# Moving operands of a decoder layer's products read column by column in turn from two areas of their tile

## The chip, the cores and the metric

The kernel runs on one core of a Trainium2 chip. A core has a matrix engine (PE in the profile; its weight loads are listed apart as PEld), a vector engine (DVE), a scalar engine (ACT), GpSimd (POOL), and a sync engine (SP) that issues most of the transfers between the chip's memory and the core's own. The metric is the device time of one execution in microseconds (us). The kernel before takes 2058.32 us, the median of three runs (2055.09, 2058.32, 2060.36).

## The reference

One layer of a decoder for 512 tokens of width 2048, everything in float32:

```
mod = SiLU(c) @ W_ada + b_ada            # six vectors: shift1, scale1, gate1, shift2, scale2, gate2
h   = RMSNorm(x) * (1 + scale1) + shift1
u   = h @ W_in                           # B, C, H of the convolution; q; k and v of three branches; gates
y_conv = B * causal_depthwise_conv3(C * H)
y_attn = gated sum of compressed, selected and sliding-window attention (8 heads, 2 key/value heads)
x   = x + gate1 * ([RMSNorm(y_conv) | RMSNorm(y_attn)] @ W_out)
h   = RMSNorm(x) * (1 + scale2) + shift2
x   = x + gate2 * (relu(h @ W1)^2 @ W2)  # W1: 2048 x 8192, W2: 8192 x 2048
out = RMSNorm(x)
```

## The kernel before

Activations lie with features on the 128 partitions and tokens along the row of a partition. A float32 product is made of three products in the format float32r: each operand is split into a rounded part and the rest (`wh` and `wl` of the weights, index 0 and 1 of the tokens' tiles), and `mm3` issues high x high, high x low and low x high into the same accumulator. The second argument of `nc.tensor.matmul` is the stationary operand, loaded by an instruction of its own (LDWEIGHTS) before each product; the third is the moving operand, which is streamed past it.

There are three stages, and the profile names their accumulators:

- Front, accumulators `ps`: the projections of `h` by `W_in`, 512 tokens wide, each weight blob of 1024 columns giving 8 x 3 products. The loop over `steps` is the first part. Its tokens `h` (features 0 to 6) and `h_m` (7 to 15) are made while it runs: for each block of 128 features DVE forms two modulation columns by four dot products with `w_ada` blobs (`wa`), scales the tokens and subtracts (`low`). Then follow `project`, `compress` (moving operand 256 columns of a compression weight, stationary operand 66 columns), `values` (moving operand 268 weight columns) and `queries`.
- Attention, accumulators `s`, `pt`, `pv`, and `pw` for the convolution's half of `W_out` (`out_conv`, 512 tokens), which fills gaps between them.
- Output projection and feed-forward, accumulators `pf`. Both feed-forward products use a scheme of seven products instead of eight over halves of 256 tokens; `run` issues 8 x 3 products, 256 tokens wide, per operand. The weight operands are rounded by ACT and their rest is formed by DVE in the tiles `hl`, three in a ring, one operand ahead of PE. In the second feed-forward product the results are added into `xt` (`gather`); when the sixth of eight feature groups is done, `add_residual` multiplies `xt` by gate2 and adds the stored residual, and the last two groups are added with the gate (`update`).

Every instruction passes through `Order.record`, so the profile puts all of them on one line, L123; they are told apart by tile names. `Order.emit` plans each of the three stages with a list scheduler: a price for each instruction (`Order.price`), due times from the order of PE's products, and the readiness of operands; it writes the instructions out in planned order, and each engine then runs its own in that order. For a float32r product the price is `max(0.109, 0.0015 + n * self.column)` us for n columns, with 0.000441 as `column` in the front and the feed-forward, and 0.000453 in attention.

In the built program the tiles of tokens start at multiples of 128 bytes of a partition's row. The weight tiles `wh`, `wl` of the front and `kw` of the output projection do so too; the tiles `hl`, `gt` and `sg`, where they hold feed-forward weights, start 64 bytes off such a multiple.

Of the kernel before, what the change touches and what calls it, by code (L numbers as in the profile page):

```python
# [16 lines left out]
P = 128  # L17
# [25 lines left out]
M_SH1, M_SC1, M_G1, M_SH2, M_SC2, M_G2 = range(6)  # L43


class Order:
# [47 lines left out]
    def price(self, eng, op, out, ins, kw):  # L94
# [199 lines left out]
def hybrid_layer(ctx: ExitStack, tc: tile.TileContext, a, out):  # L294
# [146 lines left out]
    def row_bcast(bank, total, width, dst):  # L441
# [5 lines left out]
        if dst is not None:  # L447
            nc.scalar.activation(dst, ps[:, :n * P], AF.Copy)
# [97 lines left out]
    def rope(dst, ps):  # L546
# [7 lines left out]
        nc.vector.tensor_tensor(out=dst, in0=t[:, 0], in1=t[:, 1], op=OP.add)  # L554
        yield 0.65

    def rope_split(dst, ps, scale):
        t = temp(name="rs2")
        yield from rope(t, ps)
# [69 lines left out]
    for s, (name, k) in enumerate(steps[:-1]):  # L629
# [7 lines left out]
        if s < 3:  # L637

            for ww, j in ((wh, 0), (wl, 0), (wh, 1)):
                for n, c in enumerate(cols):  # L640
                    nc.tensor.matmul(ps[n], ww[:, c], hs[k][:, j], start=first and ww is wh and j == 0,
                                     stop=last and j == 1)
# [89 lines left out]
    def project(src, tiles):  # L732
        ps = bank()
        for half in range(2):
            wh, wl = ahead.pop() if ahead else weights(src(half))
            for j in range(8):
                k = half * 8 + j
                s = slice(j * P, (j + 1) * P)
                mm3(ps, wh[:, s], wl[:, s], tiles[k][:, 0], tiles[k][:, 1], k == 0, k == NK - 1)
# [16 lines left out]
    def compress(which, src):  # L756
# [26 lines left out]
        for blk in range(8):  # L783
            wh, wl = w
            hi, lo = parts[blk // 4]
            for j in range(4):
# [4 lines left out]
                mm3(pc[:66, :256], ch, cl, wh[:, s], wl[:, s], l == 0, l == 31)  # L791
# [91 lines left out]
    def values(g):  # L883
        pv = [both[i] for i in (4, 6, 7, 5)] if g else [bank() for _ in range(NQ)]
        for n, blk in enumerate(range(4) if g == 0 else (2, 3, 1, 0)):
# [3 lines left out]
            for j in range(4):  # L889
                k = blk * 4 + j  # L890
                s = slice(j * 268, (j + 1) * 268)
                for t in range(NQ):
                    c = slice(t * P, (t + 1) * P)
                    mm3(pv[t][:, :268], hs[k][:, 0, c], hs[k][:, 1, c], wh[:, s], wl[:, s],
                        n + j == 0, (n, j) == (3, 3))
# [44 lines left out]
    def queries(g):  # L940
        pq = [bank() for _ in range(NR)]
        for k in range(NK):
# [4 lines left out]
            for n in range(NR):  # L947
                s = slice((k % 2 * NR + n) * P, (k % 2 * NR + n + 1) * P)
                mm3(pq[n], wh[:, s], wl[:, s], hs[k][:, 0], hs[k][:, 1], k == 0, k == NK - 1)
# [51 lines left out]
    def out_conv(m):  # L1001
        if m % 4 < 2:
            x1.append(slot(name="x1")[:, :1024].rearrange("p (c j t) -> p c j t", c=2, j=2))
            order.keep(x1[-1])
            for j in range(2):
                nc.sync.dma_start(out=x1[-1][:, :, j],
                                  in_=a["xt"][m // 4 * 2 + j, :, m % 2].rearrange("p (c t) -> p c t", c=2))
        ps = next(pws)
        wh, wl = oc.pop() if oc else weights(a["w_oc"][m])
        with lane(2):  # L1010
            for k in range(8):
                s = slice(k * P, (k + 1) * P)
                mm3(ps, wh[:, s], wl[:, s], mix[k][:, 0], mix[k][:, 1], k == 0, k == 7)
# [4 lines left out]
    def attention(g, qb):  # L1018
# [86 lines left out]
        for r in range(NR):  # L1105
            nc.scalar.activation(ya[g * NR + r][:, qc], pv[:, r * P:(r + 1) * P], AF.Copy)
# [28 lines left out]
    row_bcast(lambda: next(turned), tot, 1024, ra)  # L1135
# [99 lines left out]
    for k in range(8):  # L1235
        wh, wl = oa[k] if k < 2 else hilo(hl_tile(16), raw_blob(a["w_oa"][k]))
        for i in range(8):
            s = slice(i * P, (i + 1) * P)
            mm3(pm[i], wh[:, s], wl[:, s], mixa[k][:, 0], mixa[k][:, 1], k == 0, k == 7)
# [18 lines left out]
    def late_out(hf):  # L1258
        ps = []
        for i in range(8):  # L1260
# [3 lines left out]
            for k in range(8):  # L1264
                mm3(ps[-1][:, halves[i % 2]], columns(wh, k), columns(wl, k), mixa[k][:, 0, halves[hf]],
                    mixa[k][:, 1, halves[hf]], k == 0, k == 7)
# [373 lines left out]

def _shape_constants(np):
# [8 lines left out]
    i = np.arange(P)  # L1650
# [9 lines left out]
def _layouts(np, x, c, w_ada, b_ada, norm1_g, w_in, conv_w, conv_b, cmp_pe_k, cmp_pe_v, cmp_w1_k,  # L1660
# [10 lines left out]
    def quads(w):  # L1671
# [5 lines left out]
    d["xt"] = x[0].T.reshape(NK // 2, 2, P, T).transpose(0, 2, 1, 3)  # L1677
# [12 lines left out]
          .reshape(4, 4, P, 268).transpose(0, 2, 1, 3).reshape(4, P, BLOB) for g in range(NG)]  # L1690
    d["w_v"] = np.concatenate(wv)
    d["cmp_w1"] = np.concatenate([w[0].reshape(8, 4, P, 256).transpose(0, 2, 1, 3).reshape(8, P, 1024)
# [12 lines left out]
def unpack(out):  # L1705
    return out.reshape(2, NK // 4, 2, P, 2, T // 2).transpose(0, 5, 1, 4, 2, 3).reshape(1, T, D)
# [17 lines left out]
```

## Time and profile before

The profiled execution took 2054.65 us. Its span, from the first instruction to the last, is 2052.5 us; 2.15 us lie around it.

| engine | busy us | share of the span | instructions |
|---|---|---|---|
| PE, products | 2035.8 | 99% | 14994 |
| PE, weight loads | 1911.6 | 93% | 14994 |
| DVE | 1808.5 | 88% | 2639 |
| ACT | 1023.7 | 50% | 1505 |
| POOL | 174.4 | 8% | 288 |
| DMA, both queues of data | | 69.4% of 16 engines | 139888 packets |

| part of the span | what runs |
|---|---|
| 0 to 545 us | front |
| 545 to 718 us | attention, with `out_conv` between |
| 718 to 808 us | output projection |
| 808 to 2043 us | feed-forward |
| 2043 to 2052.5 us | last norm and stores |

A PE row gives the duration of a product from its start until its result has drained, and the next one starts long before that. The time that a product takes of PE is therefore read from start to start: for a row of the timeline that merges n equal products, the start of the next row less its own start, divided by n.

### The profile page before, as it was taken

To read this page: it belongs to the slowest core of one execution; us is meant where nothing else is said; L and a number is where in the kernel's file an instruction comes from. 1 tells how busy PE (TensorE), PEld (TensorE's weight loads), DVE (VectorE), ACT (ScalarE), POOL (GpSimd) and SP (SyncE) were. 2 spreads that over 40 slices of the span, in tenths; PEclk is the share of its full clock that TensorE was granted. 3 is DMA by queue.
4 is the path that set the end of the run, shared out by engine and by line. 5 is a ranking of instruction groups with operands and counts; after the bars stand their busy time and mean duration, and the time that the engine had idled before them with its cause. 6 is when DMAs were issued, how large, how long until landed. Compare 5 with 4: busy or idle time off the path is not lost.

```text
span 2052.5 us, 37822 instructions
## 1 busy us (share of the span) xinstructions
PE 2035.8 (99%) x14994; PEld 1911.6 (93%) x14994; DVE 1808.5 (88%) x2639; ACT 1023.7 (50%) x1505; POOL 174.4 (8%) x288
## 2 busy tenths in 40 slices
PE   8999999999999999999999999999999999999998
PEld 6888888888988889999999999999999999999998
DVE  8989988889999578988888888898889999999997
ACT  5432433223577336766666666666543333334354
POOL 0000000000000001132232232221000000000000
PEclk9999999999999999999999999999999999999999
DMA  9886679887310384598888888878866466377582
GB/s 376 334 338 233 239 277 319 297 290 284 114 63 32 105 322 179 169 284 254 276 250 260 275 258 251 274 228 306 298 235 234 138 250 241 130 262 283 169 253 96
DMA packets 140641, 486.15 MB, mean 237 GB/s; under 512 B 16944, under 2 KB 21552, under 8 KB 140464
## 3 DMA queue, kind: packets, MB, share of 16 engines
q1 hardware_dynamic: 113072, 391.44, 52.6%
q0 software_dynamic: 26816, 91.24, 16.8%
q8 instruction: 118, 1.93, 0.4%
q10 hardware_dynamic: 576, 1.05, 0.1%
q14 instruction: 59, 0.48, 0.1%
HBM read 414.46 MB, written 69.21 MB: 236 GB/s over the span
## 4 chain that ended last, share of the span: by engine, by line
PE 88%; DVE 1%; DMA 0%; ACT 0%; issue 0%; DVEq 0%; ACTq 0%
PE pf L123 65%; PE ps L123 15%; PE pw L123 4%; PE pv L123 2%; PE s L123 2%; PE pt L123 1%; DMA raw<-in_cmp_w 0%; DVE o L123 0%; DVE wl L123 0%; DVE sw L123 0%; ACT wh L123 0%; ACT sw L123 0%; DVE ct L123 0%; ACT p L123 0%; DVEq L1720 0%
## 5 line engine op out<-in xcount | busy, mean ns | idle before, releaser
L123 PE MATMUL pf<-tk,hl 128*128 128x256 f32 x10656 | 1213.9, 276 | 0.0
L123 PEld LDWEIGHTS pf<-tk,hl 128*128 128x128 f32 x10656 | 1212.7, 188 | 0.2 <-issue 0.2
L123 ACT ACTIVATE hl<-rw 128x1024 fp32r<-128x1024 f32 x264 | 280.0, 1061 | 326.2 <-PE pf L123 310.3
L123 DVE TENSOR_TENSOR hl<-rw,hl 128x1024 fp32r<-128x1024 f32 x264 | 322.1, 1221 | 41.9 <-ACT hl L123 41.6
L123 ACT ACTIVATE hl<-sg 128x1024 fp32r<-128x1024 f32 x183 | 194.2, 1061 | 223.1 <-PE pf L123 210.7
L123 ACT ACTIVATE wh<-raw 128x1024 fp32r<-128x1024 f32 (+1 forms) x106 | 112.7, 1063 | 257.2 <-PE ps L123 197.0
L123 PE MATMUL ps<-h_m,wh 128*128 128x512 f32 x720 | 223.6, 390 | 0.0
L123 DVE TENSOR_TENSOR hl<-sg,hl 128x1024 fp32r<-128x1024 f32 x153 | 187.0, 1223 | 33.6 <-ACT hl L123 32.2
L123 PE MATMUL ps<-h,wh 128*128 128x512 f32 x560 | 171.7, 392 | 2.3 <-ACT h L123 2.3
L123 PEld LDWEIGHTS ps<-h_m,wh 128*128 128x128 f32 x720 | 134.5, 188 | 27.7
L123 DVE TENSOR_TENSOR wl<-raw,wh 128x1024 fp32r<-128x1024 f32 (+1 forms) x106 | 129.9, 1225 | 23.8 <-ACT wh L123 22.7
L123 PE MATMUL ps<-h_m,wl 128*128 128x512 f32 x360 | 140.3, 390 | 0.0
L123 DVE CUSTOM_DVE_ANT_0 t<-wa,cs,acc 128x1024 bf16<-128x1024 f32 x96 | 122.9, 1280 | 13.7 <-DMA wa<-in_w_ada 12.9
L123 PEld LDWEIGHTS ps<-h,wh 128*128 128x128 f32 x560 | 105.2, 189 | 25.6 <-ACT h L123 3.9
L123 DVE CUSTOM_DVE_ANT_0 t<-wa,cs,vec 128x1024 bf16<-128x1024 f32 x96 | 122.8, 1280 | 4.8 <-DMA wa<-in_w_ada 3.9
L123 DVE TENSOR_TENSOR sg<-sg,rw 128x1024 f32<-128x1024 f32 x92 | 112.5, 1223 | 2.2
L123 PE MATMUL ps<-h,wl 128*128 128x512 f32 x280 | 106.4, 392 | 0.0
L123 POOL DMA_DIRECT2D g<-gt x180 | 96.7, 547 | 95.7 <-issue 52.2
L123 DVE TENSOR_TENSOR xt<-xt,pf 128x512 f32<-128x512 f32 x128 | 86.0, 682 | 15.0 <-PE pf L123 15.0
L123 PE MATMUL pw<-mix,wh 128*128 128x512 f32 x256 | 84.8, 400 | 0.0
L123 POOL DMA_DIRECT2D rw<-in_w_f x30 | 26.3, 876 | 659.8 <-DVE sg L123 619.1
L123 PEld LDWEIGHTS ps<-h_m,wl 128*128 128x128 f32 x360 | 67.6, 188 | 14.0
(242 smaller groups left out, 2282.2 us busy)
## 6 DMA issues: line engine op xcount, KB each, us to landing
rw<-in_w_f SPq DMA_DIRECT2D x260, 512.0 KB, 4.6
wa<-in_w_ada SPq DMA_DIRECT2D x192, 512.0 KB, 6.4
tk<-g SPq DMA_DIRECT2D x114, 512.0 KB, 6.1
g<-gt POOLq DMA_DIRECT2D x180, 256.0 KB, 6.9
raw<-in_w_conv SPq DMA_DIRECT2D x32, 512.0 KB, 4.7
rw<-in_w_f POOLq DMA_DIRECT2D x30, 512.0 KB, 6.0
sg<-in_w_f POOLq DMA_DIRECT2D x30, 512.0 KB, 5.4
raw<-in_w_kv SPq DMA_DIRECT2D x16, 512.0 KB, 5.3
```

The costliest lines, as they stand in the source:

```text
L123: x.i, x.eng, x.call = len(self.nodes), eng, (lambda: real(*args, **kw))
```

## The change

**What is read in turn.** Two helpers rewrite access patterns. `weave(ap, m)` reads a row of 2m columns as 0, m, 1, m+1, 2, m+2 and so on; `plainly(ap, m)` gives the other operand the same three dimensions and leaves its order as it is. With m = 64 (`W_A`) a group of 128 columns is read in turn from two areas 256 bytes apart, with 128 (`W_F`) a group of 256 from two areas 512 bytes apart, with 134 (`W_V`) the 268 columns of `values` from two areas 536 bytes apart. `mm3` has a new argument m: the moving operands are woven, the accumulator is written straight on. So the token order of a result is not that of its operand, and the rest of the change keeps track of it.

Of the 14640 float32r products 14280 are woven: 1920 of the front with 512 columns, 384 of `out_conv` with 512, 192 of the output projection with 512; 384 of `values` with 268; 192 of `compress` with 256; 384 of the output projection with 256; and 10824 of the feed-forward with 256. Products of scores, of probabilities with values, transposes and sums are as before. No product is added or removed, and no transfer.

**What follows the order.** The host stores x, the value weights and the first compression weights in another column order and sends the residual in a second copy (`xr`); the masks of attention follow. `rope`, where it feeds attention, adds its two halves with a strided read (12 additions of 512 columns on DVE); 32 copies of 128 columns on ACT and one of 512 turn the attention output and its norm factors. `add_residual` reads the stored residual with a step of 64 elements: where 16 instructions of 2 x 256 columns stood on DVE, 32 of 256 columns stand now. The host puts the output in order.

**The planner's price.** For a product whose moving operand has an innermost count of 2 it is now `max(0.1117, 0.0015 + n * 0.000421)`, for others the floor is 0.1117 too.

```diff
+W_A, W_F, W_V = 64, 128, 134
+def weave(ap, m):
+    names = " ".join("xyz"[:len(ap.shape) - 2])
+    return ap.rearrange(f"p {names} (a b i) -> p {names} a i b", b=2, i=m)
+def plainly(ap, m):
+    names = " ".join("xyz"[:len(ap.shape) - 2])
+    return ap.rearrange(f"p {names} (a i b) -> p {names} a i b", b=2, i=m)
...
-            return (0.109 if op == "transpose" else max(0.109, 0.0015 + n * self.column)), 0.2
+            column = 0.000421 if list(ins[1].ap)[-1][1] == 2 else self.column
+            return (0.109 if op == "transpose" else max(0.1117, 0.0015 + n * column)), 0.2
...
-    def mm3(ps, lh, ll, rh, rl, start, stop, more=False):
+    def mm3(ps, lh, ll, rh, rl, start, stop, more=False, m=0):
+        if m:
+            ps, rh, rl = plainly(ps, m), weave(rh, m), weave(rl, m)
         nc.tensor.matmul(ps, lh, rh, start=start, stop=False, skip_group_check=more)
...
-    def rope(dst, ps):
+    def rope(dst, ps, turned=False):
...
-        nc.vector.tensor_tensor(out=dst, in0=t[:, 0], in1=t[:, 1], op=OP.add)
+        a_, b_ = t[:, 0], t[:, 1]
+        if turned:
+            dst, a_, b_ = (v.rearrange(pat, b=2, i=W_A) for v, pat in (
+                (dst, "p (a b i) -> p a b i"), (a_, "p (a i b) -> p a b i"), (b_, "p (a i b) -> p a b i")))
+        nc.vector.tensor_tensor(out=dst, in0=a_, in1=b_, op=OP.add)
...
-                mm3(ps[n], wh[:, c], wl[:, c], hs[k][:, 0], hs[k][:, 1], first, last)
+                mm3(ps[n], wh[:, c], wl[:, c], hs[k][:, 0], hs[k][:, 1], first, last, m=W_A)
...
-            nc.scalar.activation(ya[g * NR + r][:, qc], pv[:, r * P:(r + 1) * P], AF.Copy)
+            nc.scalar.activation(plainly(ya[g * NR + r][:, qc], W_A), weave(pv[:, r * P:(r + 1) * P], W_A), AF.Copy)
...
-            mm3(ps[:, c], columns(wh, base + k), columns(wl, base + k), t[:, 0], t[:, 1], first and k == 0, last and k == n - 1, True)
+            mm3(ps[:, c], columns(wh, base + k), columns(wl, base + k), t[:, 0], t[:, 1], first and k == 0, last and k == n - 1, True, W_F)
...
             for j in range(2):
-                x = xt[2 * q + u][:, :, j]
-                nc.vector.scalar_tensor_tensor(out=x, in0=x, scalar=col(M_G2, 4 * q + 2 * j + u),
-                                               in1=r[:, :, j],
-                                               op0=OP.mult, op1=OP.add)
+                for c in range(2):
+                    x = xt[2 * q + u][:, c, j].rearrange("p (i b) -> p i b", b=4)
+                    nc.vector.scalar_tensor_tensor(out=x, in0=x, scalar=col(M_G2, 4 * q + 2 * j + u),
+                                                   in1=r[:, c, j].rearrange("p (b i) -> p i b", b=4),
+                                                   op0=OP.mult, op1=OP.add)
...
-    d["xt"] = x[0].T.reshape(NK // 2, 2, P, T).transpose(0, 2, 1, 3)
+    xt = x[0].T.reshape(NK // 2, 2, P, T).transpose(0, 2, 1, 3)
+    d["xt"] = xt.reshape(NK // 2, P, 2, T // P, P)[..., _stored(np, W_A)].reshape(xt.shape)
+    d["xr"] = xt.reshape(NK // 2, P, 2, 2, T // 2)[..., _in_turn(np, W_F)].reshape(xt.shape)
```

PE's products keep their order but for how attention's gaps are filled. On DVE the new prices move rows; two places matter for what follows. The first is the front, near the tokens of the fifth feature block: `wl` is the rest of a weight blob, `ISA t,acc` and `ISA t,mod` are dot products with `w_ada`, `h<-t,h` is the block's low part. Before:

```order
L123 TENSOR_TENSOR wl<-raw,wh 128x1024
L123 ISA t,acc<-wa,cs,vec 128x1024
L123 ISA acc 128x1
L123 ISA t,mod<-wa,cs,acc 128x1024
L123 ISA mod 128x1
L123 TENSOR_TENSOR h<-t,h 128x512
```

In the changed kernel:

```order
L136 TENSOR_TENSOR wl<-raw,wh 128x1024
L136 ISA t,acc<-wa,cs,vec 128x1024
L136 ISA acc 128x1
L136 TENSOR_TENSOR h<-t,h 128x512
L136 ISA t,mod<-wa,cs,acc 128x1024
L136 ISA mod 128x1
```

The block's low part has moved ahead of one dot product; the work is the same. The second place is DVE in the sixth feature group of the second feed-forward product, where `add_residual` begins (`xt<-xt,mod,gt`); `hl` is the rest of a weight operand, `sg<-sg,rw` a sum of weight blobs, `xt<-xt,pf` a result added. Before:

```order
L123 TENSOR_TENSOR xt<-xt,pf 128x512
L123 SCALAR_TENSOR_TENSOR xt<-xt,mod,gt 128x2x256
L123 TENSOR_TENSOR hl_5619<-sg,hl_5619 128x1024
L123 SCALAR_TENSOR_TENSOR xt<-xt,mod,gt 128x2x256
L123 TENSOR_TENSOR sg<-sg,rw 128x1024
L123 TENSOR_TENSOR hl_5620<-sg,hl_5620 128x1024
```

In the changed kernel:

```order
L136 SCALAR_TENSOR_TENSOR xt<-xt,mod,gt 128x256 x2
L136 TENSOR_TENSOR xt<-xt,pf 128x512
L136 TENSOR_TENSOR hl_5619<-sg,hl_5619 128x1024
L136 SCALAR_TENSOR_TENSOR xt<-xt,mod,gt 128x256
L136 TENSOR_TENSOR sg<-sg,rw 128x1024
L136 TENSOR_TENSOR hl_5620<-sg,hl_5620 128x1024
```

Here the residual's instructions are half as long and twice as many, still between the `hl` rows that PE waits for; the last of the 32 stand later in the program than the last of the 16 did, in the eighth feature group.

More of the change, by code (lines that the diff above doesn't have):

```diff
@@ L446, in row_bcast @@
         ps = spread(bank, rs)
-        if dst is not None:
+        if turned:
+            nc.scalar.activation(plainly(dst, W_A), weave(ps[:, :n * P], W_A), AF.Copy)
+        elif dst is not None:
             nc.scalar.activation(dst, ps[:, :n * P], AF.Copy)
@@ L558, in rope_split @@
         t = temp(name="rs2")
-        yield from rope(t, ps)
+        yield from rope(t, ps, True)
         nc.scalar.activation(dst[:, 0], t, AF.Copy, scale=scale)
@@ L640, in hybrid_layer @@
                 for n, c in enumerate(cols):
-                    nc.tensor.matmul(ps[n], ww[:, c], hs[k][:, j], start=first and ww is wh and j == 0,
-                                     stop=last and j == 1)
+                    nc.tensor.matmul(plainly(ps[n], W_A), ww[:, c], weave(hs[k][:, j], W_A),
+                                     start=first and ww is wh and j == 0, stop=last and j == 1)
         else:
             for n, c in enumerate(cols):
-                mm3(ps[n], wh[:, c], wl[:, c], hs[k][:, 0], hs[k][:, 1], first, last)
+                mm3(ps[n], wh[:, c], wl[:, c], hs[k][:, 0], hs[k][:, 1], first, last, m=W_A)
         ready = max(ready, clock) if s < 3 else ready
@@ L738, in project @@
                 s = slice(j * P, (j + 1) * P)
-                mm3(ps, wh[:, s], wl[:, s], tiles[k][:, 0], tiles[k][:, 1], k == 0, k == NK - 1)
+                mm3(ps, wh[:, s], wl[:, s], tiles[k][:, 0], tiles[k][:, 1], k == 0, k == NK - 1, m=W_A)
             tick()
@@ L1012, in out_conv @@
                 s = slice(k * P, (k + 1) * P)
-                mm3(ps, wh[:, s], wl[:, s], mix[k][:, 0], mix[k][:, 1], k == 0, k == 7)
+                mm3(ps, wh[:, s], wl[:, s], mix[k][:, 0], mix[k][:, 1], k == 0, k == 7, m=W_F)
         x = x1[m // 4 * 2 + m % 2][:, :, m // 2 % 2]
@@ L1134, in hybrid_layer @@
     ra = accum("rc")
-    row_bcast(lambda: next(turned), tot, 1024, ra)
+    row_bcast(lambda: next(turned), tot, 1024, ra, True)
     mixa = []
@@ L1238, in hybrid_layer @@
             s = slice(i * P, (i + 1) * P)
-            mm3(pm[i], wh[:, s], wl[:, s], mixa[k][:, 0], mixa[k][:, 1], k == 0, k == 7)
+            mm3(pm[i], wh[:, s], wl[:, s], mixa[k][:, 0], mixa[k][:, 1], k == 0, k == 7, m=W_F)
     for i in range(8):
@@ L1265, in late_out @@
                 mm3(ps[-1][:, halves[i % 2]], columns(wh, k), columns(wl, k), mixa[k][:, 0, halves[hf]],
-                    mixa[k][:, 1, halves[hf]], k == 0, k == 7)
+                    mixa[k][:, 1, halves[hf]], k == 0, k == 7, m=W_F)
         for i in range(8):
@@ L1638, in hybrid_layer, with _stored, _in_turn @@
     ffn.close()
+def _stored(np, m):
+    return np.arange(2 * m).reshape(m, 2).T.reshape(-1)
+def _in_turn(np, m):
+    return np.arange(2 * m).reshape(2, m).T.reshape(-1)
 def _shape_constants(np):
@@ L1649, in _shape_constants @@
     cst[half:, C_SIN:C_SIN + T] = -sin
-    i = np.arange(P)
+    i = _stored(np, W_A)
     cst[:, C_MASK:C_MASK + P] = np.where(i[None, :] <= i[:, None], 0.0, NEG)
@@ L1689, in _layouts @@
                           w_in[:, 5632 + 12 * g:5632 + 12 * g + 12]], axis=1)
-          .reshape(4, 4, P, 268).transpose(0, 2, 1, 3).reshape(4, P, BLOB) for g in range(NG)]
+          [:, _stored(np, W_V)].reshape(4, 4, P, 268).transpose(0, 2, 1, 3).reshape(4, P, BLOB) for g in range(NG)]
     d["w_v"] = np.concatenate(wv)
-    d["cmp_w1"] = np.concatenate([w[0].reshape(8, 4, P, 256).transpose(0, 2, 1, 3).reshape(8, P, 1024)
+    d["cmp_w1"] = np.concatenate([w[0][..., _stored(np, W_F)].reshape(8, 4, P, 256).transpose(0, 2, 1, 3).reshape(8, P, 1024)
                                   for w in (cmp_w1_k, cmp_w1_v)])
@@ L1705, in unpack @@
 def unpack(out):
-    return out.reshape(2, NK // 4, 2, P, 2, T // 2).transpose(0, 5, 1, 4, 2, 3).reshape(1, T, D)
+    import numpy as np
+    once = _in_turn(np, W_F)
+    full = np.empty_like(out)
+    full[..., once[once][once]] = out
+    return full.reshape(2, NK // 4, 2, P, 2, T // 2).transpose(0, 5, 1, 4, 2, 3).reshape(1, T, D)
 def kernel(**inputs):
```

11 lines of the change are left out of this document (6 added, 5 removed).

## The prediction

> **What bounds the kernel now.** I read the page first: the engines' busy time, the chain of work that ended last, and the costliest group.
>
> ```profile
> span 2052.5 us, 37822 instructions
> ...
> PE 2035.8 (99%) x14994; PEld 1911.6 (93%) x14994; DVE 1808.5 (88%) x2639; ACT 1023.7 (50%) x1505; POOL 174.4 (8%) x288
> ...
> PE 88%; DVE 1%; DMA 0%; ACT 0%; issue 0%; DVEq 0%; ACTq 0%
> ...
> L123 PE MATMUL pf<-tk,hl 128*128 128x256 f32 x10656 | 1213.9, 276 | 0.0
> ```
>
> PE is busy 99% of the span, is 88% of the chain, and the largest group has no idle time before it. So the time is the sum of PE's start-to-start times. Those come from three places: the chain in order of time, and the timeline of PE in the front (512 columns) and at the output projection (256 columns).
>
> ```profile
> 888.47 1152.83 PE pf L123 x10136
> ```
>
> The feed-forward: 1152.83 us for 10136 products of 256 columns, **113.7 ns** each.
>
> ```profile
> 199.74 0.62 PE L123 MATMUL ps<-h_m,wh 128*128 128x512 f32 x2
> ...
> 203.82 0.39 PE L123 MATMUL ps<-h,wh 128*128 128x512 f32 x1
> ```
>
> From the first row's start to the last row's there are 18 products of 512 columns: 4.08 / 18 = **226.7 ns** each.
>
> ```profile
> 772.87 2.88 PE L123 MATMUL pf<-mixa,gt 128*128 128x256 f32 x24
> 775.59 8.80 PE L123 MATMUL pf<-mixa,kw 128*128 128x256 f32 x72
> 784.23 2.60 PE L123 MATMUL pf<-mixa,hl 128*128 128x256 f32 x21
> 786.67 0.50 PE L123 MATMUL pf<-ones,sacc 128*128 128x1 f32 x4
> ```
>
> The same moving tiles and the same shape, only the weight tile differs. With `gt` a product takes 2.72 / 24 = 113.3 ns, with `kw` 8.64 / 72 = 120.0 ns. `kw` starts at a multiple of 128 bytes, as the tokens do; `gt` 64 bytes off one. So a product's time depends on where the next weights are loaded from while it streams: **the weight load and the moving operand get in each other's way**, by at least 6.7 ns per product when both are in the same phase. Front and `out_conv` are in that phase, the feed-forward is not.
>
> The Trainium skill (TensorE: Matmul & The Clock Gate, Step-by-step: what each phase is for) says that PE has two independent read ports, so that loading the next weights takes nothing from the running product. These two rows differ from it: 113.3 against 120.0.
>
> ```profile
> 659.70 0.71 PE L123 MATMUL s<-kslc,q 128*128 128x32 f32 x5
> 660.25 0.66 PE L123 MATMUL pt<-vec,p 128*128 128x128 f32 x4
> 660.66 0.82 PE L123 MATMUL s<-kslc,q 128*128 128x32 f32 x6
> 661.34 0.48 PE L123 MATMUL pw<-mix,wl 128*128 128x512 f32 x1
> ```
>
> Products of only 32 columns take (0.55 + 0.68) / 11 = **111.8 ns**: that is the weight load alone, the floor for any product with 128 columns of weights.
>
> **The price of a woven product.** No row shows a moving operand read in turn, so I bound it. A product of 512 columns in the same phase takes 226.7 ns, one of 256 takes 120.0: the second 256 columns, with no weight load behind them, cost 106.7 ns, 0.417 ns per column. Without interference 512 columns would then cost 213.4 ns and a fixed part; 120.0 - 106.7 = 13.3 ns is interference and fixed part together, of which at least 6.7 is interference. So the gain per product of 512 columns, if reading in turn removes the interference, lies between 6.7 and 13.3 ns; I take the middle, **10 ns**. The other end of the unknown is no gain, and below that a loss (rivals). Products of 256 columns would stream in 106.7 ns and a fixed 3 to 4, less than the weight load, so 111.8 ns is what they get: **1.9 ns** off 113.7. For the lower end I keep 109 ns, which is 4.7 off, the reading in which the weight load too is slowed in the narrow rows; for the upper, nothing off, in which 113.7 is already a weight load.
>
> ```profile
> 417.71 0.41 PE L123 MATMUL ps<-wh,h_m 128*128 128x268 f32 x2
> ...
> 420.67 0.41 PE L123 MATMUL ps<-wh,h_m 128*128 128x268 f32 x2
> ```
>
> The 268 columns of `values`: 24 products in 2.96 us, 123.3 ns; streamed they are 268 x 0.417 + 3.5 = 115.3, a gain of 8.0 ns. `compress`:
>
> ```profile
> 225.58 0.40 PE L123 MATMUL ps<-sw,chi 128*66 128x256 f32 x2
> ...
> 226.28 0.40 PE L123 MATMUL ps<-sw,chi 128*66 128x256 f32 x2
> ```
>
> Six products in 0.70 us, 116.7 ns; with 66 weight columns the stream is the bound, 110.2, a gain of 6.5.
>
> The sum on PE:
> - 512 columns: 1920 + 384 + 192 = 2496 products x 10 ns = 25.0 us
> - feed-forward, 10824 x 1.9 = 20.6 us
> - `values`, 384 x 8.0 = 3.1 us; `compress`, 192 x 6.5 = 1.2 us
> - output projection, 256 columns: 144 with `kw` x 8.2 = 1.2 us, 240 others from about 116 (2.44 / 21 in the `hl` row) x 4.2 = 1.0 us
>
> Together **52.1 us**. By the Trainium skill (TensorE: Matmul & The Clock Gate, Back-to-back issue gap) a lone product of 512 columns is spaced 512 / 2.4 + 2.5 = 215.8 ns; the estimate for the first term by it would be 27.2 us instead of 25.0, and nothing above hangs on it.
>
> **What takes some of it back.** PE can only be faster where its operands are earlier too. Two places are tight.
>
> The front: the tokens `h` come from DVE, which waits for the `w_ada` blobs (12.9 us in the first of its two groups of dot products).
>
> ```profile
> L123 DVE CUSTOM_DVE_ANT_0 t<-wa,cs,acc 128x1024 bf16<-128x1024 f32 x96 | 122.9, 1280 | 13.7 <-DMA wa<-in_w_ada 12.9
> ```
>
> ```profile
> 50.00:100.00 50.00, 50.00 (x222) 41.40 (x221) 49.01 (x78) 23.02 (x31) 0.00 (x0) 1.00 0.88 332
> 100.00:150.00 50.00, 50.00 (x222) 41.41 (x221) 45.48 (x71) 19.17 (x23) 0.00 (x0) 1.00 0.88 342
> ```
>
> DVE is busy 49.0 of 50 us (fourth number), the DMA engines 88%. Their work per feature block isn't changed, so they set the pace if PE catches up. How far ahead are they?
>
> ```profile
> 149.82 0.69 DVE L123 TENSOR_TENSOR h_m<-t,h_m 128x512 fp32r<-128x512 f32 x1
> ```
>
> The last block's low part is done at 150.51. Its first product is the one that starts at 152.82:
>
> ```profile
> 152.82 0.62 PE L123 MATMUL ps<-h_m,wh 128*128 128x512 f32 x2
> ```
>
> That is 2.3 us ahead. In the 20 steps of 24 products before it, which go back to 44 us at 226.7 ns each, PE would gain 20 x 24 x 10 ns = 4.8 us. It can use 2.3; **2.5 us are lost**. The order rows of the front move a low part past one dot product but take no work out. Where the cover of 2.3 us is kept by earlier transfers the loss is 0, where DVE falls back it is 4.8.
>
> The end of the feed-forward: DVE again.
>
> ```profile
> 1800.00:1850.00 50.00, 50.00 (x443) 50.00 (x442) 47.05 (x52) 19.63 (x19) 0.00 (x0) 1.00 0.68 251
> 1850.00:1900.00 50.00, 50.00 (x443) 50.00 (x442) 49.36 (x58) 20.64 (x20) 0.00 (x0) 1.00 0.80 286
> 1900.00:1950.00 50.00, 50.00 (x443) 50.00 (x443) 50.00 (x68) 19.12 (x18) 0.89 (x1) 1.00 0.51 169
> 1950.00:2000.00 50.00, 50.00 (x443) 50.00 (x442) 48.49 (x77) 28.36 (x42) 4.28 (x5) 1.00 0.85 254
> 2000.00:2043.00 43.00, 42.67 (x375) 42.50 (x373) 34.27 (x67) 25.01 (x51) 0.00 (x0) 1.00 0.21 71
> ```
>
> In 200 us DVE idles 5.1 us, none of it from 1900 to 1950. It runs its rows in order, so whatever stands ahead of an `hl` row delays PE. Here `add_residual` grows from 16 to 32 instructions:
>
> ```profile
> L123 DVE SCALAR_TENSOR_TENSOR xt<-pf,mod,xt 128x256 f32<-128x256 f32 x58 | 26.0, 478 | 4.7 <-PE pf L123 4.7
> ...
> L123 DVE SCALAR_TENSOR_TENSOR xt<-xt,mod,gt 128x512 f32<-128x512 f32 x16 | 11.9, 747 | 0.0
> ...
> L123 DVE TENSOR_TENSOR t<-rt 128x512 f32<-128x512 f32 x12 | 8.0, 687 | 0.0
> ...
> L123 DVE TENSOR_TENSOR ct<-kc,cw 128x512 f32<-128x512 f32 x2 | 2.1, 1048 | 0.0
> ```
>
> At 478 ns for 256 columns the 32 cost 15.3 us, 3.4 more than 11.9. The read with a step makes it worse: the `ct` row, which reads one input with a step, takes 1048 ns where a plain addition takes 687, a factor of 1.53; with it 32 x 731 = 23.4 us, 11.5 more. Against that stand the 5.1 us idle and, after 2000 us, some more; and PE's own gain there, 1.9 of 113.7 over 200 us, is 3.3 us that DVE would have to follow. Loss between 0 and 11 us, **I take 5**. The 12 strided additions of `rope` cost 12 x 0.36 = 4.3 us of DVE in the front and lie beside PE's products; the copies on ACT lie beside an engine that is half idle.
>
> Net 52.1 - 2.5 - 5 = **44.6 us**. The profiled execution took 2054.65 us (2.15 around its span) and would become 2010.0. It lies 3.7 us below the median of the runs, 2058.32, so the forecast for the median is **2013 us**.
>
> **The rivals.**
> - *Only the wide products gain* (0.13). 113.7 in the feed-forward may already be its weight load; the chain of PEld supports it (1911.6 us busy, without a gap there). Then 25.0 + 3.1 + 1.2 + 1.2 - 3 = 27.5 us: 2031. Against it: the narrow rows load the same weights in 111.8.
> - *Nothing is removed* (0.07): the interference hangs on the weights' phase alone, and reading in turn keeps the phase, since 256 and 512 bytes are multiples of 128. Then 2058, and up to 5 more from DVE's end. If the ports were independent, as the Trainium skill's rule above has it, there would be nothing to remove either and the time the same; the `kw` row speaks against that.
> - *Slower: collision on every column* (0.05), in the feed-forward. Two areas read in turn advance by one column per 2 x 0.417 = 0.83 ns each, nearly the pace of a weight load (111.8 / 128 = 0.87 ns per column). In lockstep the two reads meet always or never. If always, the 64 bytes that keep them apart now are worth nothing, and 256 columns take the 120.0 ns of the `kw` row: 10824 x 6.3 = 68 us, 2058 + 68 = 2126. It outweighs the 29 us of the other terms from 2.7 ns per product on.
> - *Slower: a read with a step costs PE what it costs DVE* (0.03): factor 1.53 on 2496 x 226.7, 10824 x 113.7 and 960 others at about 118 ns is 1.0 ms, 3070 us. What speaks for it is the `ct` row alone; no product in this trace has a step. The Trainium skill (SBUF — State Buffer, Door 1: The DMA port swizzle) says so too: lines of 16 bytes, at least two hits per line for full rate, and a penalty for each access that crosses to another line; read in turn, each access does. No run here shows it for PE.
> - *More* (0.02): the feed-forward falls to 109 ns, 30 us more, 1983.
>
> **How the numbers follow.** The forecast has the other 0.70; its own bounds are 2496 x 3.3 ns = 8 us either way, and the two losses at 0 or at 16: about 1997 to 2026. With the first rival and its few us of loss, 2036, I have 0.83; so 1996 to 2036. Faster by over 0.3% (6 us, about what a measurement of this kernel can tell from no change): 0.70 + 0.13 + 0.02 = 0.85; within: 0.07; slower: 0.08.
>
> **What would show it.** PE start to start: 216 to 218 ns for 512 columns in the front, 111 to 112 in the feed-forward, and the `kw` products no slower than `gt`. DVE near 100% from 1800 us on with PE waits of some us for `hl`, and waits of PE for `h` before 155 us. The residual's rows at 0.48 or at 0.73 us say which end of the loss holds. I am wrong if the feed-forward stays at 113 to 114 ns (2031), if 512 columns stay at 227, or if any woven product gets slower.

## The result and the profile after

The changed kernel takes **2034.77 us**, the median of four runs (2032.49 to 2041.11), beside 2056.70 us for the kernel before in the same comparison: a ratio of 0.9898, 95% interval 0.9869 to 0.9927. Measured once more on another chip (e14 below) it takes 2033.32 us against 2055.68: 0.9890, interval 0.9875 to 0.9905. So the change is worth about 22 us. The forecast was 2013, a gain of 45, so half of it came. 2034.77 lies outside the 1997 to 2026 that the forecast gave itself; it lies inside 1996 to 2036, the range that takes in the first rival.

The profiled execution took 2032.49 us. Its page, the span, the engines' busy time and the chain by engine:

```profile
span 2030.7 us, 37909 instructions
...
PE 1987.3 (98%) x14994; PEld 1890.8 (93%) x14994; DVE 1810.7 (89%) x2655; ACT 1019.9 (50%) x1505; POOL 174.8 (9%) x288
...
PE 78%; DVE 12%; DMA 5%; issue 3%; ACT 1%; SPq 0%; POOL 0%; DVEq 0%; ACTq 0%; POOLq 0%
```

PE is busy for 48.5 us less than before (2035.8), but the span is only 21.8 us shorter: PE now stands idle for 43.4 us instead of 16.7. The chain says where to look. PE has fallen from 88% of it to 78%, DVE has risen from 1% to 12% and the transfers from 0% to 5%.

First the products, read as in the prediction: the timeline of PE in the front (start, duration, group, count), where 42 products of 512 columns start from the first row up to the last; the output projection; and the longest piece of the chain.

```profile
194.68 0.59 PE L136 MATMUL ps<-h_m,wh 128*128 128x512 f32 x2
...
203.74 0.59 PE L136 MATMUL ps<-h_m,wh 128*128 128x512 f32 x2
```

```profile
761.64 2.84 PE L136 MATMUL pf<-mixa,gt 128*128 128x256 f32 x24
764.32 8.20 PE L136 MATMUL pf<-mixa,kw 128*128 128x256 f32 x72
772.36 2.84 PE L136 MATMUL pf<-mixa,hl 128*128 128x256 f32 x24
```

```profile
908.23 956.85 PE pf L136 x8565
```

512 columns: 9.06 / 42 = **215.7 ns** (226.7 before). `kw`: 8.04 / 72 = 111.7 ns (120.0), and `gt`: 2.68 / 24 = 111.7 (113.3): the difference between the two phases is gone. The feed-forward: 956.85 / 8565 = **111.7 ns** (113.7). So every product got the price that was forecast, or a better one.

Then the place where the time is lost. The timeline of PE where the front ends and attention begins; in brackets stand the idle time before a group and who ended it:

```profile
518.00 0.46 PE L136 MATMUL s<-kslc,q 128*128 128x160 f32 x3
522.74 1.57 PE L136 MATMUL s<-kslc,q 128*128 128x160 f32 x6 [4.28 <-ACT vr L136]
...
525.03 0.63 PE L136 MATMUL pw<-mix,wl 128*128 128x512 f32 x1
525.46 0.63 PE L136 MATMUL pw<-mix,wh 128*128 128x512 f32 x1
537.05 0.93 PE L136 MATMUL s<-kslc,q 128*128 128x160 f32 x3 [10.95 <-DVE pc L136]
```

The timeline of DVE at the same time. `t<-wa,cs` is a dot product with a `w_ada` blob, `q<-t,q` is the last work on the queries, `s<-s,cst` the first mask operation of attention, for which the scores `s` above had been ready since 518.5:

```profile
517.88 1.29 DVE L136 CUSTOM_DVE_ANT_0 t<-wa,cs,vec 128x1024 bf16<-128x1024 f32 x1
...
525.52 1.28 DVE L136 CUSTOM_DVE_ANT_0 t<-wa,cs,acc 128x1024 bf16<-128x1024 f32 x1
...
533.19 2.49 DVE L136 SCALAR_TENSOR_TENSOR q<-t,q 128x512 fp32r<-128x512 f32 x4
535.60 0.29 DVE L136 TENSOR_TENSOR s<-s,cst 128x128 f32<-128x128 f32 x1
```

And the same place in the kernel before:

```profile
536.47 0.68 DVE L123 SCALAR_TENSOR_TENSOR q<-t,q 128x512 fp32r<-128x512 f32 x1
540.26 0.30 DVE L123 TENSOR_TENSOR s<-s,cst 128x128 f32<-128x128 f32 x1 [3.11 <-PE s L123]
```

Before, DVE waited 3.11 us for PE there; that was all the room it had. Now PE is done 21.8 us earlier (last product of the front at 517.88 us instead of 539.64), but DVE still has 17 us of the front in its in-order queue, and attention starts only 4.7 us earlier. The two largest waits of DVE in the front, after and then before (total, times, longest; `wl <- ACT wh` is the wait for a rounded weight blob):

```profile
DVE t L136 <- DMA wa<-in_w_ada: 24.5, 22, 3.0
DVE wl L136 <- ACT wh L136: 11.6, 18, 2.3
```

```profile
DVE wl L123 <- ACT wh L123: 22.4, 30, 1.8
DVE t L123 <- DMA wa<-in_w_ada: 13.4, 14, 2.5
```

The one got shorter and the other longer by as much: DVE waits 36 us for the two before and after. So the `w_ada` transfers now hold it back too. In the chain of the changed kernel they are 10.1% of the first 545 us, and DVE's dot products 6.8%; in the chain before, no transfer of a `w_ada` blob appears there.

Last, stretches of the changed kernel (busy us of PE, PEld, DVE, ACT, POOL; granted clock; DMA share; GB/s), and the residual's group:

```profile
500.00:550.00 50.00, 34.70 (x236) 32.11 (x235) 47.25 (x101) 21.93 (x56) 0.00 (x0) 0.80 0.48 165
...
1900.00:1950.00 50.00, 47.07 (x401) 46.42 (x400) 48.98 (x70) 17.97 (x17) 2.62 (x3) 0.97 0.75 257
1950.00:2000.00 50.00, 48.36 (x431) 48.00 (x431) 49.83 (x85) 32.16 (x55) 2.55 (x3) 1.00 0.48 123
```

```profile
L136 DVE SCALAR_TENSOR_TENSOR xt<-xt,mod,gt 128x256 f32<-128x256 f32 x32 | 20.6, 673 | 0.0
```

From 500 to 550 us PE works 34.7 of 50 us, and the granted clock averages 0.80. It had dropped by the end of the first wait: the product at 525.03 us and the one at 525.46, both ahead of the long wait, start 0.43 us apart. From 1900 us on PE waits, while DVE is as full as before; the residual's rows take 673 ns, so 9.6 us more of DVE than before (32 x 0.673 against 11.9). PE at the largest of these waits:

```profile
1899.75 25.01 PE L136 MATMUL pf<-tk,hl 128*128 128x256 f32 x217
1927.10 4.55 PE L136 MATMUL pf<-tk,hl 128*128 128x256 f32 x24 [2.34 <-DVE xt L136]
1932.09 33.18 PE L136 MATMUL pf<-tk,hl 128*128 128x256 f32 x295 [0.45 <-DVE xt L136]
```

The wait costs more than its 2.34 us. The 24 products behind it take 4.54 us (4.99 from row to row, less 0.45 idle), where 24 x 111.7 ns are 2.68; from 1927.1 to 1931.6 us the granted clock is 0.62.

Where the gain went, from the starts of the same work in the traces (us; e1, e9 and e13 are experiments below):

| | before | after | e1 | e9 | e13 |
|---|---|---|---|---|---|
| last product of the front | 539.64 | 517.88 | 518.14 | 518.28 | 544.21 |
| first mask operation of attention (DVE) | 540.26 | 535.60 | 518.75 | 518.90 | 544.84 |
| first product of the output projection | 718.35 | 709.49 | 691.59 | 692.48 | 722.14 |
| first product of the feed-forward | 807.85 | 794.91 | 785.85 | 778.85 | 811.64 |
| its 2000th | 1038.88 | 1024.39 | 1020.47 | 1009.74 | 1040.01 |
| its 9000th | 1833.09 | 1806.06 | 1802.13 | 1791.40 | 1834.22 |
| end of the span | 2052.49 | 2030.72 | 2027.83 | 2015.78 | 2054.14 |

- Front: the products are worth 1920 x 10.95 = 21.0 us, `values` (123.3 to 114.2) 3.5 and `compress` (116.7 to 109.4) 1.4, together 25.9. Of these 21.8 have arrived at the last product; 4.1 are lost.
- Start of attention: of 21.8 us 4.7 are left. **17.1 lost**; in the traces of e4, e7, e10, e11 and e14, which have nearly the same rows in the front, it is 16.7 to 17.4.
- `out_conv` brings 384 x 10.95 = 4.2 us, the output projection 4.1. Both arrive: 12.9 at the first product of the feed-forward.
- Feed-forward: between its 2000th and 9000th product before needs 794.21 us, after 781.67, so 1.79 ns per product, 19.4 us for 10824. Up to the 2000th 2.0 us are lost, from the 9000th to the end 8.5.

Sum: 25.9 + 4.2 + 4.1 + 19.4 = 53.6, less 4.1 + 17.1 + 2.0 + 8.5 = 31.7, is 21.9; the spans differ by 21.8.

### The profile page after: what moved, and what is told of

It reads as the page before. It is cut to its first block, busy times and chain, and to the rows that moved or that the text cites. A ratio compares the mean times of both kernels' runs of the same rounds, so it can differ in the third digit from the quotient of the medians.

```text
span 2030.7 us, 37909 instructions
## 1 busy us (share of the span) xinstructions
PE 1987.3 (98%) x14994; PEld 1890.8 (93%) x14994; DVE 1810.7 (89%) x2655; ACT 1019.9 (50%) x1505; POOL 174.8 (9%) x288
## 4 chain that ended last, share of the span: by engine, by line
PE 78%; DVE 12%; DMA 5%; issue 3%; ACT 1%; SPq 0%; POOL 0%; DVEq 0%; ACTq 0%; POOLq 0%
PE pf L136 55%; PE ps L136 14%; PE pw L136 4%; DMA wa<-in_w_ada 3%; DVE t L136 3%; DVE hl L136 2%; DVE xt L136 2%; PE pv L136 2%; PE s L136 2%; DVE wl L136 1%; PE pt L136 1%; DVE sg L136 1%; DVE rt L136 1%; DMA g<-gt 1%; DMA raw<-in_cmp_w 1%
## 5 line engine op out<-in xcount | busy, mean ns | idle before, releaser
L136 PE MATMUL pf<-tk,hl 128*128 128x256 f32 x10656 | 1196.5, 275 | 8.2 <-DVE t L136 3.0
L136 PEld LDWEIGHTS pf<-tk,hl 128*128 128x128 f32 x10656 | 1193.4, 192 | 10.0 <-issue 3.6
L136 PE MATMUL ps<-h_m,wh 128*128 128x512 f32 x720 | 215.5, 380 | 0.0
L136 PE MATMUL ps<-h,wh 128*128 128x512 f32 x560 | 165.2, 382 | 3.4 <-ACT h L136 2.6
L136 DVE TENSOR_TENSOR sg<-rw 128x1024 f32<-128x1024 f32 x61 | 74.4, 1219 | 7.2 <-DMA rw<-in_w_f 5.5
```

What stands on the lines that cost most here:

```text
L136: x.i, x.eng, x.call = len(self.nodes), eng, (lambda: real(*args, **kw))
```

## The experiments

The theory: **at the start of attention DVE, with the front's work in its queue, has become the bound, and PE's gain in the front stops there.** The rivals: the wait belongs to attention or to the new token order; the planner's new prices made the order worse; the loss is elsewhere, at the end. Each run stands beside the kernel before on the same chip. The ratio is to the kernel before, with its 95% interval.

### e1 and e2: sixteen dot products out of the front

```
-NLATE = 8
+NLATE = 16
```

The last `NLATE` columns of the modulation are left to `late_ada`, which computes them in the output projection. First on the changed kernel (e1), then on the kernel before (e2).

> The changed kernel, with 16 instead of 8 modulation columns (M_G2) left to the second, later group, so 16 dot products of 1.28 us and their 16 w_ada blobs leave the front: 20.5 us of DVE. Theory (the front's gain was lost because DVE's in-order queue was still 17 us behind when PE had done the front): the first mask operation of attention starts near 520 us instead of 535.6, PE's waits for DVE pc (11.0 us) and ACT vr (4.3) there go, and the time falls by 8 to 15 us, to 2020-2027. The dots come back between 700 and 850 us, where DVE has about 25 us free, so a little may be lost there. Rival (the wait at the start of attention is that of the attention chain itself, or of the reordered token operands): the wait stays and the time is within 3 us of 2035.

Measured: 2029.69 us, ratio 0.9874 (0.9859 to 0.9888). Attention starts at 518.75 us, so the wait is gone and 16.9 us are won there; the output projection starts 17.9 us earlier. But the feed-forward starts only 9.1 us earlier. These two stretches of e1 show why:

```profile
750.00:800.00 50.00, 44.97 (x373) 43.76 (x373) 48.67 (x86) 32.05 (x60) 5.93 (x11) 0.97 0.73 272
800.00:850.00 50.00, 44.41 (x387) 43.49 (x387) 47.89 (x76) 38.22 (x67) 5.61 (x9) 1.00 0.46 132
```

PE idles 10.6 us, with DVE at 48 of 50: the dot products have only moved the jam. The mechanism is as the theory has it; the time missed its range, because I gave the place that takes the work too little weight.

> The same edit in the kernel before: 16 dot products leave the front. Theory: there DVE was done 3 us ahead of PE, so PE set the start of attention and nothing is to be gained: within 4 us of 2057. Rival (dot products in the front cost time whatever PE does): the same gain as in the changed kernel, 8 to 15 us.

Measured: 2075.10 us, ratio 1.0096 (1.0079 to 1.0113). Attention starts at 540.47 us instead of 540.26, so there was nothing to gain there, as expected. But the run is 20 us slower, not within 4: PE loses 17 between 718 and 884 us, beside the moved dot products. So moving work off DVE in the front is worth nothing while PE is the later one, and costs where it lands.

### e3: the front read plainly again

```
-                mm3(ps[n], wh[:, c], wl[:, c], hs[k][:, 0], hs[k][:, 1], first, last, m=W_A)
+                mm3(ps[n], wh[:, c], wl[:, c], hs[k][:, 0], hs[k][:, 1], first, last)
```

(and so in `project`, in `queries` and in the first three steps)

> The changed kernel with the products of w_kv, w_cv, w_conv, w_q and the other 512-column products of h read plainly again (2112 products; the token order of what they produce is then not the one the later steps assume, so the output is in a mixed order). They cost 10.9 us per thousand more, 23 us in all on PE. Theory: PE then ends the front near 541 us and DVE near 535, so only about 5 us of the 23 are lost: 2037 to 2044. Rival (the gain of the front arrives whole and the missing 30 us went elsewhere): 2035 + 23 = 2058.

Measured: 2038.96 us, ratio 0.9916 (0.9900 to 0.9933). The products are back at 227 ns and PE has 21 us more to do (1920 products; the 2112 of the expectation count the output projection's 192 too), yet the time rises by 4 to 6 us. In the changed kernel, then, the largest single term of the front is worth only about 5 us. The rival's 2058 is out. The order of the engines was not as expected, though: PE's last product of the front starts at 534.57 us and DVE's first mask operation at 540.55. DVE is still the later one, by 6 us instead of 17.

### e4: the residual read plainly

```
-                for c in range(2):
-                    x = xt[2 * q + u][:, c, j].rearrange("p (i b) -> p i b", b=4)
-                    nc.vector.scalar_tensor_tensor(out=x, in0=x, scalar=col(M_G2, 4 * q + 2 * j + u),
-                                                   in1=r[:, c, j].rearrange("p (b i) -> p i b", b=4),
-                                                   op0=OP.mult, op1=OP.add)
+                x = xt[2 * q + u][:, :, j]
+                nc.vector.scalar_tensor_tensor(out=x, in0=x, scalar=col(M_G2, 4 * q + 2 * j + u),
+                                               in1=r[:, :, j], op0=OP.mult, op1=OP.add)
```

> The changed kernel with add_residual as before: 16 plain instructions of 747 ns instead of 32 strided ones of 673 (the residual is then added to the tokens of another order). DVE has 9.6 us less to do between 1800 and 1970 us. Theory: the 5.4 us that PE loses against its own pace after 1918 us shrink to 1 or 2: 2030 to 2032. Rival (DVE is full there with the weights' halves and updates, and PE's own gain is what it cannot follow): at most 1.5 us gained.

Measured: 2029.85 us, ratio 0.9873 (0.9858 to 0.9887), 3.5 us below e14; the two intervals overlap. By the trace PE loses 5.3 us from the 9000th product of the feed-forward to the end instead of 8.5; the expectation had 1 or 2 left, so it met the time and not the loss. About a third of the loss goes with the strided rows here; e15 says it once more, and e7 shows that the rest can't simply be put down to PE's pace.

### e5 and e6: the moved dot products beside out_conv

```
-NLATE = 8
+NLATE = 16
...
+    late_ada(8, 4)
     while m < NK:
         out_conv(m)
         m += 1
```

> The changed kernel with 16 instead of 8 columns of M_G2 taken out of the front, as in e1, but 8 of them are computed at the end of the attention stage, beside the last products of out_conv (630 to 700 us, DVE 34 to 40 of 50 us busy in e1), and only the other 8 in the output projection as before. Theory (e1 won 18 us at the start of attention and gave back 13 because 41 us of dot products stood between 690 and 870 us): the 18 us stay: 2016 to 2021. If the end of the feed-forward, which DVE bounds, takes more of it back, up to 2023. Rival (the 13 us of e1 were not the dot products' doing): as e1, 2030.

Measured: 2027.24 us, ratio 0.9861 (0.9846 to 0.9875): not enough. Attention starts at 517.63 us, but then PE waits once for 10.89 us. DVE just before, and PE after it (`x<-pw` evicts a product of `out_conv`):

```profile
693.52 1.28 DVE L136 CUSTOM_DVE_ANT_0 t<-wa,cs,vec 128x1024 bf16<-128x1024 f32 x1
...
694.93 1.28 DVE L136 CUSTOM_DVE_ANT_0 t<-wa,cs,acc 128x1024 bf16<-128x1024 f32 x1
...
696.14 0.74 DVE L136 SCALAR_TENSOR_TENSOR x<-pw,mod,x 128x512 f32<-128x512 f32 x1
```

```profile
697.03 1.20 PE L136 MATMUL pw<-mix,wh 128*128 128x512 f32 x2 [10.89 <-DVE x L136]
```

Six dot products stood between two evictions, so both of PE's result banks stayed full. It is the order of DVE's queue there that cost this: in e9 below, with two dot products fewer but never more than three between two evictions, PE has no such wait.

> The same edit in the kernel before. Theory: nothing to gain at the start of attention, where PE was the later one, and nothing lost in the output projection: within 4 us of 2055. Rival (the rearrangement is worth something by itself, whatever PE's pace): 2040 or less.

Measured: 2064.41 us, ratio 1.0045 (1.0031 to 1.0059): attention starts at 540.18 us, no gain there, and the output projection 9.4 us later than before, as in e5. The expectation missed that loss.

### e7: the feed-forward read plainly again

```
-            mm3(ps[:, c], columns(wh, base + k), ..., last and k == n - 1, True, W_F)
+            mm3(ps[:, c], columns(wh, base + k), ..., last and k == n - 1, True)
```

> The changed kernel with the products of the feed-forward read plainly (10824 of 256 columns; what they write is then in another order than the residual, so the output's tokens are mixed). Theory: a product goes from 111.8 back to 113.7 ns, 22 us in all, and of the 5.4 us lost at the end about 5 come back, since PE is slower there: 2035 + 16 to 22 = 2050 to 2057. Rival (DVE, not PE, sets the pace of the feed-forward): less than 8 us slower.

Measured: 2054.76 us, ratio 0.9991 (0.9982 to 1.0001): 21 us slower than the changed kernel, as expected, and no faster than before. Without the 1.8 ns of the feed-forward's products, then, nothing of the gain is left. But the loss at the end does not come back, as the expectation had it. From the 9000th product to the end the trace has 228.4 us, against 219.4 in the kernel before at the same price of a product: 9.0 us are lost with products as slow as before. (The traced execution is the slowest of the ten of e7, 4 us over the median; its attention starts 3 to 5 us later than in the other traces with this front.)

### e8, e10 and e11: which readings in turn are fast

```
+def even_odd(ap):
+    names = " ".join("xyz"[:len(ap.shape) - 2])
+    return ap.rearrange(f"p {names} (i b) -> p {names} b i", b=2)
...
-                mm3(ps[n], wh[:, c], wl[:, c], hs[k][:, 0], hs[k][:, 1], first, last, m=W_A)
+                mm3(ps[n], wh[:, c], wl[:, c], even_odd(hs[k][:, 0]), even_odd(hs[k][:, 1]), first, last)
```

> The changed kernel with the 512-column products of the front reading even columns first, then the odd ones, instead of two areas in turn (tokens come out in a mixed order). What is looked at is the time from start to start. If it is the turn between two areas that frees PE: 227 ns, as plain. If any reading that is not contiguous does: 216. If a read with a step costs PE as it costs DVE (673 against 478 ns): above 300.

In e10 the areas are 4 columns long (`m=4` for `m=W_A`), in e11 16.

> The changed kernel with the two areas of the front's 512-column products only 4 columns (16 bytes) long instead of 64: column 0, 4, 1, 5, 2, 6, 3, 7, 8, 12 and so on (tokens come out in a mixed order). If what made even-odd slow (452 ns in e8) is that two reads that follow each other fall into the same few bytes, this is slow too in part, between 216 and 452. If it is the long run with a step of 2, then 216.

> The same with areas of 16 columns (64 bytes). If the distance of 64 bytes is enough, 216 ns per product as with 64 columns; if two areas must be further apart, more.

Measured: 2466.49, 2034.79 and 2035.07 us. The timelines of PE, of e8 (27 products start from the first row up to the last) and of e10 (32):

```profile
299.44 0.63 PE L141 MATMUL ps<-h_m,wl 128*128 128x512 f32 x1
...
311.68 0.63 PE L141 MATMUL ps<-h_m,wl 128*128 128x512 f32 x1
```

```profile
179.63 0.59 PE L136 MATMUL ps<-h_m,wh 128*128 128x512 f32 x2
...
186.54 0.38 PE L136 MATMUL ps<-h_m,wl 128*128 128x512 f32 x1
```

Even-odd: 12.24 / 27 = **453 ns**, twice a plain product. Areas of 4 columns: 6.91 / 32 = 215.9 ns, as with 64; areas of 16: 216 too. So not every reading that isn't contiguous is fast, and a jump by itself isn't slow either: alternating between places 16 bytes apart costs no more than between places 256 bytes apart, and going through the tile in steps of 8 bytes halves the rate.

### e9 and e13: the dot products spread, and the same edit on the kernel before

```
-NLATE = 8
+NLATE = 15
...
+    late_ada(7, 3)
     while m < NK:
         out_conv(m)
         m += 1
```

> The changed kernel with 15 instead of 8 columns of M_G2 taken out of the front (14 dot products, 17.9 us of DVE), 7 of them computed at the end of the attention stage with 3 instead of 4 tiles for the w_ada blobs, so that at most three of them stand between two evictions of out_conv (in e5 six stood there, and PE waited 10.9 us behind them). Theory: the 18 us of the start of attention are kept and the wait of e5 is gone: 2016 to 2021. Rival (out_conv at the end of attention has no room for them whatever their order): as e5, 2027.

Measured: **2017.65 us**, ratio 0.9823 (0.9810 to 0.9837), the fastest version that computes the reference. DVE at the start of attention:

```profile
515.40 0.68 DVE L136 SCALAR_TENSOR_TENSOR q<-t,q 128x512 fp32r<-128x512 f32 x1
518.90 0.30 DVE L136 TENSOR_TENSOR s<-s,cst 128x128 f32<-128x128 f32 x1 [2.81 <-PE s L136]
```

DVE is again ahead of PE, by 2.81 us, as it was before the change. The 17 us arrive at the output projection (692.48 against 709.49 us) and 15 of them at the end. One thing the runs don't separate: with each dot product its `w_ada` blob of 512 KB leaves the front too, so whether DVE's work or the transfers that it waits for set its pace there stays open.

> The edit of e9 in the kernel before: 15 instead of 8 columns of M_G2 out of the front, 7 of them at the end of the attention stage with 3 tiles. Theory (the 17 us of e9 are the front's gain of the changed kernel let through, and no gain of the edit itself): within 5 us of 2055, and attention starts at 540 us as before. Rival (taking dot products out of the front is worth 17 us whatever PE's pace): 2038 or less. If the first, the two gains do not add: change alone 21 us, edit alone about 0, both 37.

Measured: 2055.91 us, ratio 1.0000 (0.9991 to 1.0009). Attention starts at 544.84 us, 4.6 later than before and not at 540 as expected; 3.1 of these are there by 53 us, and why wasn't traced. DVE waits for PE there, as before. The change alone brings 22 us, this edit alone nothing, both together 37. The edit has no gain of its own; it lets the front's gain through.

### e12 and e14: the planner's prices

```
-            column = 0.000421 if list(ins[1].ap)[-1][1] == 2 else self.column
-            return (0.109 if op == "transpose" else max(0.1117, 0.0015 + n * column)), 0.2
+            return (0.109 if op == "transpose" else max(0.109, 0.0015 + n * self.column)), 0.2
```

> The changed kernel with the planner's prices of before (0.000441 us per column for all products, at least 0.109), so that the order is planned for a slower PE while the products stay as they are. Theory (the front's DVE has too much to do, whatever the order): the start of attention stays near 536 us and the time within 4 us of 2035. Rival (the plan by the new prices put DVE's work of the front too late): attention starts before 530 us, 2028 or less.

> The changed kernel itself, once more beside the kernel before on this chip, because its first interval (0.9869 to 0.9927) does not tell it from e12 (0.9876) and e4 (0.9873). If the old prices of e12 are better than the new ones, this stays at 2034 and more; if they make no difference, this comes out at 2029 to 2032.

Measured: e12 2028.99 us, ratio 0.9876 (0.9863 to 0.9890); e14 2033.32, 0.9890 (0.9875 to 0.9905). With the old prices attention starts at 533.90 us: PE loses its lead inside the front instead (its last product starts at 527.91), for the same DVE. The time is 6 us below 2035, 2 more than expected. e14 came out between its two expectations, and the intervals overlap, so whether the new prices cost a few us stays open. They don't account for 17.

### e15: e9 with the residual read plainly

> e9 with add_residual plain as in e4 (the residual is added to tokens of another order). In e9 PE still loses 6 us against its own pace after 1900 us. Theory (half of it is add_residual's extra 9.6 us of DVE, as the trace of e4 has it): 2 to 4 us faster than e9, 2013 to 2016. Rival (all of it is add_residual): 2011. Rival (none): 2017.

Measured: 2013.46 us, ratio 0.9796 (0.9782 to 0.9809), 4.2 us below e9, just over what was expected and more than nothing. From the 9000th product to the end PE loses 5.7 us instead of 8.3 by the traces. The rest stays, and DVE was full there before the change too. But these are not two causes that add up: e7, with the strided rows and PE as slow as before, loses 9.0, and e12, with the strided rows, the fast PE and the old prices, 5.9. The planned order of DVE's rows differs between these runs and counts as well.

## Why the prediction was wrong

- **The price of a product: right.** Forecast 10 ns for 512 columns, 1.9 for the feed-forward, 8.0 for `values`, 6.5 for `compress`; measured 10.95, 1.8, 9.1 and 7.3. The sum was 52.1 us, and 53.6 came. The estimate by the Trainium skill (TensorE: Matmul & The Clock Gate, Back-to-back issue gap) for a lone product, 215.8 ns, agrees with 215.7. The rule of two independent ports in the Trainium skill (TensorE: Matmul & The Clock Gate, Step-by-step: what each phase is for) doesn't: `kw` fell from 120.0 to 111.7 ns with the same weights and the same amount to read. The 111.8 ns held for these products (111.7), but it is not a floor for any product with 128 columns of weights: the `pt` row in the view that was read for it has 0.41 / 4 = 103 ns.
- **"Two places are tight": this is the step that failed.** In the front I set DVE's lead over PE against PE's gain only as far as the step at 153 us, where the 2.3 us of lead were real and were used up (that step starts 3.6 us earlier, against 5.3 gained on PE; of the 1.7 lost, forecast 2.5, 0.8 are a later first product and 0.8 one wait for `h` at 76.85 us). Then I let PE's gain of the next 350 us through as if DVE had no say in it: the strided additions of `rope` were to lie beside PE's products. (They cost 12 x 0.10 = 1.2 us, 786 against 687 ns in the mean, not 4.3.) The term was 2.5 us; in its place stand 4.1 lost within the front and 17.1 at its end. The row that says so is in the trace of before, and I did not look it up: DVE reaches attention with 3.11 us to spare, against the 22 that PE was to gain by then. e1, e9 and e13 show it: the wait goes when DVE's dot products and their blobs go, and taking them away is worth nothing where PE is the later one.
- **The average misled.** I quoted DVE's share in the stretches up to 150 us, 49.0 and 45.5 of 50; from 250 to 500 us of the kernel before it is 40 to 45, which looks like room. But DVE runs in order and waits for `w_ada`; its idle time in between is no reserve (24.5 us of such waits in the front now, 13.4 before, with as much less waiting for `wh`).
- **The end of the feed-forward: right place, size within the bounds.** Forecast 5 us within 0 to 11; 8.5 were lost. The residual's instruction takes 673 ns, between the 478 and the 731 of the two bounds. PE waited for `xt` (2.8 us) and for ACT's `hl` (1.6) rather than for DVE's `hl`, and ran slower behind a wait. What the bounds had as one cause is more: without the strided rows about 3 us of the loss go (e4, e15); what makes the rest stays open, since it is there with PE as slow as before too (e7).
- **The first rival, that only the wide products gain, gave 2031 and came near the time for the wrong reason.** The narrow ones gained (e7), and it was most of the wide ones' gain in the front that was lost.
- **The rivals on the slow side fell for this change.** A reading that slows PE does exist: even-odd, by a factor of 2.0 (e8). The rule of the Trainium skill (SBUF — State Buffer, Door 1: The DMA port swizzle: lines of 16 bytes, two hits per line for the full rate) fits neither way here: even-odd hits each line twice in a row and runs at half rate; areas of 4 columns change the line at each read and run at full rate.

Open: 2.0 us at the start of the feed-forward; 1.6 of the 4.1 us in the front (0.8 are a later first product, 1.7 are idle time of PE between 50 and 500 us, 3.1 instead of 1.4; the rest was not traced); most of the 8.5 us at the end; and what the new prices cost.

## What to carry to other kernels

Before you add up what the bound engine gains, walk through the stage boundaries and read, at each, how far the next engine is ahead there: that lead, and what this engine itself becomes faster, is all you can win up to that point, whatever the shares of busy time say. Here the lead was 3.11 us, and 4.7 of 21.8 us were won. If it is smaller than the gain, plan the second edit with the first: here one was worth 22 us alone, the other nothing, and both 37. And look where the moved work lands, row by row: sixteen dot products cost 17 us in one place, fourteen nothing where they were spread.

## What the runs showed of the hardware

- Two areas of the moving operand read in turn cost PE less than a contiguous read: 215.7 ns instead of 226.7 for 512 columns, and with it the phase of the weight tile no longer matters (`kw` and `gt` both 111.7 ns). Areas of 4, 16 and 64 columns do equally well in the front (215.9, 216 and 215.7 ns).
- Even columns first, then odd ones: 453 ns for 512 columns, 0.88 ns per column. Why a step of 8 bytes costs half the rate, and a jump of 16 bytes and back no more than one of 256, was not settled.
- A strided input has no single price on DVE. The residual's rows take 673 ns for 256 columns, 1.41 times the 478 of the plain row that I had taken for comparison (which reads one input from an accumulator); the strided additions of `rope` take 786 instead of 687 ns in the mean, a factor of 1.14, and single ones between 685 and 893. Both are less than the 1.53 of the row that I had taken as the bound.
- A wait of PE can cost more than its length. Between the waits of 4.28 and 10.95 us at the start of attention, products of 512 columns started 0.43 us apart instead of 0.216. That cost little, as PE had to wait for DVE anyway: from the first mask operation to the first product of the output projection are 173.9 us, and 173.6 in e9, which has no such wait. Behind the wait of 2.34 us at 1927 us, 24 products took 4.54 us instead of 2.68, with a granted clock of 0.62.
